# The first MLP product of the context tokens: token tiles as stationary operand, W1 moving in split tiles of 512 columns, results turned by PE transposes

## Chip, core and metric

The kernel runs on one core of a Trainium2 chip. The metric is device microseconds of one launch. The kernel before took 2586.35 us as the median of three runs (2584.51 to 2587.87). A difference of about 0.2%, some 5 us, is what a measurement of this kernel can tell from no change.

## What is computed

One layer of a diffusion backbone on 128 context tokens (one tile of 128 rows) and 2048 latent tokens (16 tiles). A DeltaNet and gMLP mixer comes first; it is not touched. Behind it stands the MLP, for context and latent tokens with the same weights:

```python
def block(x, s0, mod, n_chunks, ...):
    ...
    x = x + ga1 * o
    h = rmsnorm(x, norm_ffn_l) * (1.0 + sc2) + sh2
    x = x + ga2 * (jnp.square(jax.nn.relu(h @ w_ff1_l)) @ w_ff2_l)
    return x, s_new
```

`w_ff1` (W1) is 1024 x 4096 and `w_ff2` is 4096 x 1024, all in 32-bit floats. The change is about `square(relu(h @ w_ff1))` for the 128 context rows.

## The kernel before

All engines work on tiles of 128 partitions by 512 floats (256 KB), nearly all from one pool of 49 buffers (`wp`). A product that must be exact to about 32 bits is made of three matmuls (`mm3`, lines 238 to 244): each operand is split into a rounded part H (a cast on ScalarE, ACT) and a rest L (a subtraction on VectorE, DVE), and H by H, H by L and L by H are added up in PSUM. Lines 242, 243 and 244 of the profile are these three. PSUM is eight banks of 512 floats, handed out by `bank()`.

The first MLP product of the latent tokens is a two-by-two block scheme with seven products instead of eight, over `ORDER = (1, 5, 6, 7, 3, 2, 4)`. The 16 latent tiles form two halves of 8; a half's activations lie in seven `hop` tiles of 2 MB, one for each product, which move through the PE as the 512-wide operand; `hop_next` loads one in two transfers of 1 MB. W1 goes through the PE as the stationary operand. A `Unit` holds 256 columns of W1 (four raw tiles `raw[i, kh]` of 256 KB, read in rows of 512 bytes) and makes seven `step(o)`s of 12 matmuls each. There are 16 units for each half. `seq` lists the 224 steps; the first two and last two units of a half run interleaved. At position `p` the program emits the loads of the unit at `p + 14`, the splits of its weights at `p + 6` (`LEAD`), and the step of `p`. `half` is the position at which the second half begins; around it the seven `hop` tiles are exchanged, each as soon as the PE has used the old one for the last time. SyncE (SP) issues all these transfers in one queue, in order.

The second half takes the context tokens along: `weights_at`, for four of the seven products (`SINGLE`), emits `Unit.single`, which multiplies the unit's raw W1 tiles, unsplit, with the 128 context columns `x0` as the moving operand. A `T.matmul` on unsplit 32-bit floats runs as two matmul instructions, so the 256 calls are 512 instructions of 128 columns in the profile (line 1646). `single_out` then takes relu on ACT (line 1652), squares on DVE and stores `z_d[0]`. The result has W1's columns on the partitions, as the second product wants it.

A scheduler orders each engine's instructions when the program is built; `h2_steps` (transposes of line 889) run in the first half.

Behind the second half comes the MLP's second product (`products`, matmuls on `zH` and `zL`). Its first loads are issued from 16 positions before the end of `seq`.

Of the kernel before, what the change touches and what calls it, by code (L numbers as in the profile page):

```python
# [12 lines left out]
AF = mybir.ActivationFunctionType  # L13
ALU = mybir.AluOpType
# [3 lines left out]
P = 128  # L18
D = 1024
KT = D // P  # L20
# [34 lines left out]
NV = 7  # L55
LEAD = 6
ORDER = (1, 5, 6, 7, 3, 2, 4)
SINGLE = {6: (0, 0), 7: (1, 0), 2: (0, 1), 4: (1, 1)}
NK = DFF // P // 2
AHEAD = 3  # L60
WINDOWS = [2.46, 0.03, -0.51, 1.06, -1.61, 18.16, 17.58, 18.3,
# [4 lines left out]
def hybrid_step(  # L66
# [7 lines left out]
    V, A, G, T = nc.vector, nc.scalar, nc.gpsimd, nc.tensor  # L74
    load = nc.sync.dma_start
    store = nc.sync.dma_start
# [10 lines left out]
    def f32(ap):  # L87
        return ap.bitcast(F32)
# [25 lines left out]
    z_d = [dp.tile([4 if a else 1, P, 2, NK, P], F32, name=f"z{a}_d") for a in range(5)]  # L114
# [4 lines left out]
    ident = cp.tile([P, P], F32, name="ident")  # L119
# [69 lines left out]
    def raw_w(src, pool=None, tag="w"):  # L189
        t = (pool or wp).tile([P, 512], F32, tag=tag, name="raw")  # L190
        load(out=t, in_=src)
        return t

    def split_w(raw, scale=None, pool=None, tag="w"):

        h = (pool or wp).tile([P, 512], F32R, tag=tag, name="wH")
        lo = (pool or wp).tile([P, 512], F32R, tag=tag, name="wL")
        if scale is not None:
            A.activation(h, raw, AF.Copy, scale=scale)
            V.scalar_tensor_tensor(out=lo, in0=raw, scalar=scale, in1=f32(h), op0=ALU.mult, op1=ALU.subtract)  # L200
            return h, lo
        A.copy(h, raw)
        V.tensor_tensor(out=lo, in0=raw, in1=f32(h), op=ALU.subtract)
        return h, lo
# [24 lines left out]
    def w512(name, dt=F32):  # L229
        return wp.tile([P, 512], dt, tag="w", name=name)  # L230
# [7 lines left out]
    def mm3(ps, trip, first=True, last=True, more=False):  # L238

        n = len(trip)  # L240
        for i, (lh, ll, rh, rl) in enumerate(trip):
            T.matmul(ps, lh, rh, start=first and i == 0, stop=False, skip_group_check=more)  # L242
            T.matmul(ps, lh, rl, start=False, stop=False, skip_group_check=more)  # L243
            T.matmul(ps, ll, rh, start=False, stop=last and i == n - 1, skip_group_check=more)  # L244
# [51 lines left out]
    with ExitStack() as ph:  # L296
# [8 lines left out]
        def pt():  # L305
            return ppt.tile([P, 512], F32, tag="pt", name="pt", bufs=3)
# [7 lines left out]
        for d in range(2):  # L314
            m = p1.tile([P, P], F32, tag=f"mcum{d}", name=f"mcum{d}", bufs=1)
# [33 lines left out]
        def mod_sum(raws, psum):  # L349

            pm = psum()
            for k in range(KT):
                T.matmul(pm[0:2, :], scond[:, k, :], raws[k], start=k == 0, stop=k == KT - 1)
            row = pf.tile([2, 512], F32, tag="first", name="first", bufs=2)
            A.copy(row, pm[0:2, :])
            return row
# [45 lines left out]
        r0 = mod_sum(m0, pm1)  # L402
# [15 lines left out]
        ps = pt()  # L418
# [4 lines left out]
        for t in BLOCKS[0]:  # L423
            x = p1.tile([P, D], F32, tag="x", name="x", bufs=3)
# [368 lines left out]
        for bi in range(len(BLOCKS)):  # L793
# [8 lines left out]
            for n, (gi, h) in enumerate(order):  # L802
                u = us[n] if bi == 0 and n < 3 else feature_tile(blk, bi, gi, h)
# [150 lines left out]
    def hop_next():  # L954
        g, o = hop_order.pop(0)
        hop[g, o] = t = hop_tile(F32R, o in ORDER[:2])
        for k in range(0, 4, 2):
            load(out=f32(t)[:, k : k + 2], in_=hop_d[g, o][:, k : k + 2])


    with ExitStack() as ph:
# [246 lines left out]
        units = [unit(t, 0) for t in range(NT)] + [unit(t, 1) for t in [0] + list(range(NT - 1, 0, -1))]  # L1208
# [218 lines left out]
        for i, u in enumerate(units):  # L1427
            w = p2 if i <= NT else p3
# [7 lines left out]
            n = len(u["prep"])  # L1436
# [6 lines left out]
            if i >= NT:  # L1443
                at(i, lambda u=u: o_loads(u))
                first, second = o_steps(u)
# [21 lines left out]
        for j, st in enumerate(flat[:NF]):  # L1467
            g, k = divmod(j, KT + 1)
# [53 lines left out]
    def bank():  # L1522
        return psq.tile([P, 512], F32, tag="f", name="f", bufs=8)

    def add(out, a, b, op=ALU.add):
        V.tensor_tensor(out=out, in0=a, in1=b, op=op)  # L1526

    def split4(src, name="w"):

        h = wp.tile([P, 4, P], F32R, tag="w", name=name + "H")  # L1530
        lo = wp.tile([P, 4, P], F32R, tag="w", name=name + "L")
        A.copy(h, src)  # L1532
        add(lo, src, f32(h), ALU.subtract)
        return h, lo

    def as4(t):
        return t.rearrange("p (a d) -> p a d", a=4)


    NP = DFF // 256  # L1540
    x0 = []

    class Unit:

# [37 lines left out]
        def product(self, o, onto=None):  # L1582
            if onto is None:
                self.ps[o] = bank()
            (h, lo), m = self.w[o], hop[self.g, o]
            mm3(self.ps[onto or o], [(h[:, kp, :], lo[:, kp, :], m[:, :, 0, kp, :], m[:, :, 1, kp, :]) for kp in range(4)],
                first=onto is None, more=onto is not None)
# [50 lines left out]
                rl2(c, c)  # L1638
                self.out(1, 0, c)

        def single(self, o, ps, i, first, last):

            m, kh = SINGLE[o]
            c = (2 * i + m) * P
            for kp in range(4):
                T.matmul(ps[:, c : c + P], self.raw[m, kh][:, kp, :], x0[kh][:, kp, :], start=first and kp == 0,  # L1646
                         stop=last and kp == 3)

    def single_out(units, ps):
        n = 256 * len(units)  # L1650
        z = w512("z0")
        A.activation(z[:, :n], ps[:, :n], AF.Relu)
        add(z[:, :n], z[:, :n], z[:, :n], ALU.mult)
        for i, u in enumerate(units):
            store(out=z_d[0][0, :, :, u.jp, :], in_=z[:, i * 256 : i * 256 + 256].rearrange("p (a t) -> p a t", a=2))

    def first_load():
        for i in range(2):
            r = as4(w512("x0"))
            load(out=r, in_=h2_d[0][:, i * 4 : i * 4 + 4, :])  # L1660
            x0.append(r)


    pairs = [(9 + 2 * i, 10 + 2 * i) for i in range(4)] + [(1 + 2 * i, 2 + 2 * i) for i in range(4)]
# [23 lines left out]
    def fetch(src, name="r2"):  # L1688
        t = w512(name)
        load(out=t, in_=src)  # L1690
        return t
# [177 lines left out]
    def t_ahead(n, upto):  # L1869
        while n < len(products) and len(traws) < min(upto, NK):  # L1870
            traws.append(fetch(moving(products[n][0], len(traws)), "traw"))

    def t_next(n, k):

        if n < len(products):
            t_ahead(n, k + 4)
            tiles[n].append(t_build(traws[k], k))
            if k == NK - 1:
                traws.clear()

    def s_next(m, loads):
        if m < len(todo):
            if loads:
                raws[m] = s_load(*todo[m][1:])
            else:
                sops[m] = s_build(*raws.pop(m))
# [4 lines left out]
    units = {n: Unit(n) for n in range(2 * NP)}  # L1891
# [2 lines left out]
        seq += [(o, n, b) for o in ORDER for n in b]  # L1894
    begun = set()

    bank0 = {}

    def weights_at(p):
        if p < len(seq):  # L1900
            o, n, b = seq[p]
            units[n].weights(o)
            if n >= NP and o in SINGLE:
                first, last = o == 6 and n == b[0], o == 4 and n == b[-1]
                if first:
                    bank0[b[0]] = bank()
                units[n].single(o, bank0[b[0]], b.index(n), first, last)
                if last:
                    single_out([units[m] for m in b], bank0[b[0]])

    def loads_at(p):
        if p < len(seq) and seq[p][1] not in begun:
            begun.add(seq[p][1])
            units[seq[p][1]].loads()
# [3 lines left out]
    for p in range(LEAD):  # L1918
        if p < 5:
            hop_next()  # L1920
        weights_at(p)
    half = [p for p, e in enumerate(seq) if e[1] == NP][0]
    later = []
    for j, t in enumerate(range(8, -1, -1)):
        st = h2_steps(t, bank, lambda: w512("junk"), w512)
        p = 10 + 19 * j // 2
        later += [(p + (-4, 0, 1, 2, 4, 5)[k] if k < 6 else p + 2 * k - 6, st[k]) for k in range(len(st))]
    later.sort(key=lambda e: e[0])
    last = len(seq) - 16
    for p, (o, n, b) in enumerate(seq):  # L1930
        u = units[n]
        loads_at(p + LEAD + 8)
        weights_at(p + LEAD)
        while later and later[0][0] <= p:
            later.pop(0)[1]()
        if p == half - 20:
            first_load()
        u.step(o)
        if half - 11 <= p < half + 3 and (half - p) % 2:
            hop_next()  # L1940
        e = p - last
        if e >= 0 and e % 2:
            if e // 2 == 0:
                for m in range(AHEAD):
                    s_next(m, True)
                t_ahead(0, 4)
            elif e // 2 < 5:
                for k in range(4 * (e // 2) - 4, 4 * (e // 2)):
                    t_next(0, k)
                if e // 2 <= AHEAD:  # L1950
                    s_next(e // 2 - 1, False)
                    s_next(AHEAD + e // 2 - 1, True) if e // 2 < 3 else None
# [4 lines left out]
    for m, (n, i, u, q) in enumerate(todo):  # L1957
# [6 lines left out]
        if q == 0:  # L1964
            ps = bank()
# [6 lines left out]
        h, lo = sops.pop(m)  # L1972
        if m >= len(todo) - 4:
# [8 lines left out]
            if q == 3:  # L1982
                rest[0](ps, 0)
                ps = bank()
# [12 lines left out]
        if i in (1, 5, 6) and mm < 28:  # L1997
            while pending and mm >= pending[0][0] + 2:
                _, k, r = pending.pop(0)
# [60 lines left out]
```

## Time and profile before

| | us |
|---|---|
| median of three runs | 2586.35 |
| the profiled execution, device time | 2589.03 |
| its span, first to last instruction | 2587.1 |
| PE busy in it | 2547.4 |
| DVE busy | 1805.3 |
| ACT busy | 1221.0 |

The stages that matter: the first half of the first MLP product runs from 1246.9 us of the span on, the second half from about 1540 us to 1923 us, the second product to the end. "L1646" is line 1646 of the kernel; `f` is a PSUM bank, `hop` the activations, `wH` and `wL` split weights. A window row gives, for each engine, busy us and in brackets the number of instructions; then the granted TensorE clock as a share of the full one, the share of the time in which the DMA engines were busy, and GB/s.

### The profile page before, as it was taken

The page shows a single profiled execution, that of the slowest core. Times are in us where ns is not written, and L with a number is a line of the kernel's source. Part 1 is how long each engine was busy: PE and PEld are TensorE (multiplying, and loading weights), DVE is VectorE, ACT ScalarE, POOL GpSimd, SP SyncE. Part 2 cuts the span into 40 slices and gives each one's busy share as a digit, 9 for nine tenths or more (in the row PEclk, how much of TensorE's full clock was granted, in tenths as well). Part 3 has the DMA queues.
Part 4 walks back from the last instruction along what each step waited for, and adds up shares of the span by engine and source line. Part 5 has one row for each costly group of instructions (what it writes and reads, how often), then busy time and mean ns, then how long its engine had stood idle before and what let it go on. Part 6 is the DMA issues. An engine that isn't in the chain of part 4 may idle for free.

```text
span 2587.1 us, 44754 instructions
## 1 busy us (share of the span) xinstructions
PE 2547.4 (98%) x15556; PEld 2154.5 (83%) x15556; DVE 1805.3 (70%) x3738; ACT 1221.0 (47%) x3051; POOL 233.7 (9%) x448
## 2 busy tenths in 40 slices
PE   9999999999999999999999999999999999999998
PEld 5899998788888787788888888888888888888887
DVE  5867757766677878886678876666665557784875
ACT  4755556555555667764345543333342432342442
POOL 3112212111111111210000000000000000000000
PEclk9999999999999999999999999999999999999999
DMA  8977737644454656885868788444479979786683
GB/s 287 300 219 213 211 111 253 229 154 155 144 160 151 215 177 235 281 275 183 280 205 252 230 289 293 122 115 118 120 239 368 345 257 327 266 257 204 223 266 112
DMA packets 494695, 571.88 MB, mean 221 GB/s; under 512 B 35124, under 2 KB 297564, under 8 KB 490886
## 3 DMA queue, kind: packets, MB, share of 16 engines
q1 hardware_dynamic: 494470, 569.04, 67.8%
q8 instruction: 122, 2.00, 0.3%
q14 instruction: 103, 0.84, 0.1%
HBM read 389.23 MB, written 179.67 MB: 220 GB/s over the span
## 4 chain that ended last, share of the span: by engine, by line
PE 86%; DMA 6%; DVE 5%; ACT 2%; issue 1%; SPq 0%; POOL 0%; POOLq 0%; DVEq 0%; ACTq 0%
PE f L242 16%; PE f L244 16%; PE f L243 16%; PE pj L242 7%; PE pj L244 6%; PE pj L243 6%; PE pd L1011 4%; PE f L1646 2%; PE pm L242 1%; PE pm L244 1%; PE pm L243 1%; PE pt L626 1%; DMA QK<-qk_d 1%; DMA raw<-in_w_mod_dram 1%; DMA hop_d<-opL 1%
## 5 line engine op out<-in xcount | busy, mean ns | idle before, releaser
L242 PE MATMUL f<-hop,zH 128*128 128x512 f32 (+1 forms) x976 | 376.2, 386 | 1.2 <-ACT zH L1532 1.2
L243 PE MATMUL f<-hop,zH 128*128 128x512 f32 (+1 forms) x976 | 376.1, 386 | 0.0
L244 PE MATMUL f<-hop,zL 128*128 128x512 f32 (+1 forms) x976 | 376.1, 386 | 0.0
L242 PE MATMUL f<-hop,wH 128*128 128x512 f32 x896 | 355.2, 397 | 0.1
L243 PE MATMUL f<-hop,wH 128*128 128x512 f32 x896 | 349.0, 390 | 0.0
L244 PE MATMUL f<-hop,wL 128*128 128x512 f32 x896 | 347.9, 390 | 0.0
L1532 ACT CAST zH<-zraw 128x512 fp32r<-128x512 f32 x240 | 146.4, 620 | 284.6 <-DMA zraw<-s_d 86.9
L242 PEld LDWEIGHTS f<-hop,zH 128*128 128x128 f32 x976 | 183.3, 188 | 38.5 <-ACT zH L1532 1.6
L244 PEld LDWEIGHTS f<-hop,zL 128*128 128x128 f32 x976 | 183.3, 188 | 37.3 <-DVE zL L1526 0.4
L243 PEld LDWEIGHTS f<-hop,zH 128*128 128x128 f32 x976 | 183.3, 188 | 36.9 <-issue 0.2
L1526 DVE TENSOR_TENSOR zL<-zraw,zH 128x512 fp32r<-128x512 f32 x240 | 162.6, 687 | 72.2 <-ACT zH L1532 55.1
L244 PEld LDWEIGHTS f<-hop,wL 128*128 128x128 f32 x896 | 168.2, 188 | 35.3
L242 PEld LDWEIGHTS f<-hop,wH 128*128 128x128 f32 x896 | 168.5, 188 | 32.8 <-issue 0.5
L243 PEld LDWEIGHTS f<-hop,wH 128*128 128x128 f32 x896 | 168.5, 188 | 32.3
L242 PE MATMUL pj<-kH,wH 128*128 128x386 f32 (+2 forms) x568 | 190.5, 338 | 1.3 <-ACT junk L602 1.1
L243 PE MATMUL pj<-kL,wH 128*128 128x386 f32 (+2 forms) x568 | 189.5, 335 | 0.5 <-POOL kL L511 0.5
L244 PE MATMUL pj<-kH,wL 128*128 128x386 f32 (+2 forms) x568 | 189.7, 335 | 0.0
L185 POOL TENSOR_TENSOR r<-rsq,nhalf 128x1 f32<-128x1 f32 (+1 forms) x37 | 25.1, 679 | 1418.0 <-DVE rsq L184 1418.0
L572 DVE SCALAR_TENSOR_TENSOR cv<-pj,vec,cv 128x384 f32<-128x384 f32 (+2 forms) x164 | 87.0, 539 | 52.7 <-ACT cv L569 51.4
L242 PEld LDWEIGHTS pj<-kH,wH 128*128 128x128 f32 x568 | 107.0, 189 | 4.6 <-issue 2.6
L1532 ACT CAST wH<-s 128x512 fp32r<-128x512 f32 x96 | 59.4, 621 | 105.5 <-DVE s L1526 103.5
L243 PEld LDWEIGHTS pj<-kL,wH 128*128 128x128 f32 x568 | 107.4, 189 | 1.4 <-POOL kL L511 0.8
(410 smaller groups left out, 5703.9 us busy)
## 6 DMA issues: line engine op xcount, KB each, us to landing
zraw<-z_d SPq DMA_DIRECT2D x212, 256.0 KB
raw<-in_w_ff_dram SPq DMA_DIRECT2D x128, 256.0 KB
hop<-hop_d SPq DMA_DIRECT2D x28, 1024.0 KB
z_d<-c SPq DMA_DIRECT2D x96, 256.0 KB
zraw<-s_d SPq DMA_DIRECT2D x96, 256.0 KB
raw<-in_w_mod_dram SPq DMA_DIRECT2D x80, 256.0 KB
r<-in_w_ff_dram SPq DMA_DIRECT2D x80, 256.0 KB
s_d<-s SPq DMA_DIRECT2D x64, 256.0 KB
```

What stands on the lines that cost most here:

```text
L185: G.tensor_tensor(out=out, in0=t[:np_, :n], in1=nhalf[:np_, :n], op=ALU.pow)
L242: T.matmul(ps, lh, rh, start=first and i == 0, stop=False, skip_group_check=more)
L243: T.matmul(ps, lh, rl, start=False, stop=False, skip_group_check=more)
L244: T.matmul(ps, ll, rh, start=False, stop=last and i == n - 1, skip_group_check=more)
L572: V.scalar_tensor_tensor(out=cv[:, o : o + m], in0=ps[:, s + sh : s + sh + m], scalar=convw[:, w, j : j + 1], in1=cv[:, o : o + m], op0=AL ...
L626: T.matmul(ps[:, i * P : (i + 1) * P], kTt[:, i * P : (i + 1) * P], rhs[:, i * P : (i + 1) * P], start=True, stop=True)
L1011: T.matmul(p[:, h, :], lhs[:, h, :], rhs[:, h, :], start=True, stop=True)
L1526: V.tensor_tensor(out=out, in0=a, in1=b, op=op)
L1532: A.copy(h, src)
L1646: T.matmul(ps[:, c : c + P], self.raw[m, kh][:, kp, :], x0[kh][:, kp, :], start=first and kp == 0, stop=last and kp == 3)
```

## The change

`Unit.single`, `single_out` and `SINGLE` go, and with them line 1646. In their place the context tokens get a product of their own over the whole of W1. `first_load` now splits `x0` into H and L (four tiles that stay). `context_steps(m)` handles one 128 x 512 tile of W1, `m = 8 fb + k` (eight blocks `fb` of 512 columns, eight tiles `k` of 128 rows):

- `fetch`: load the tile from DRAM once more (rows of 2 KB), 10 positions ahead;
- `split`: cast on ACT, rest on DVE, 4 positions ahead;
- `product`: three matmuls with the context's H or L as stationary operand and the W1 tile as 512 moving columns; at `k = 7`, relu of the whole bank on ACT;
- `turn`, 2 positions later and once for each block: four PE transposes of 128 x 128 into a second bank, a square on ACT and two stores.

One `m` comes every one and a half positions, from `half - 6` on, so that the last product stands at `half + 88` of 112 positions.

```diff
-        def single(self, o, ps, i, first, last):
-            m, kh = SINGLE[o]
-            c = (2 * i + m) * P
-            for kp in range(4):
-                T.matmul(ps[:, c : c + P], self.raw[m, kh][:, kp, :], x0[kh][:, kp, :], ...)
-    def single_out(units, ps):
-        A.activation(z[:, :n], ps[:, :n], AF.Relu)
-        add(z[:, :n], z[:, :n], z[:, :n], ALU.mult)
...
     def first_load():
         for i in range(2):
             r = as4(w512("x0"))
             load(out=r, in_=h2_d[0][:, i * 4 : i * 4 + 4, :])
-            x0.append(r)
+            h, lo = split4(r, "x")
+            x0.extend((h[:, k, :], lo[:, k, :]) for k in range(4))
+
+    def context_steps(m):
+        fb, k = divmod(m, KT)
+        u = first_tile
+        def fetch():
+            u["raw", m] = raw_w(w_ff1[0, k * P : (k + 1) * P, fb * 512 : fb * 512 + 512])
+        def split():
+            u["w", m] = split_w(u.pop(("raw", m)))
+        def product():
+            if k == 0:
+                u["ps"] = bank()
+            mm3(u["ps"], [x0[k] + u.pop(("w", m))], first=k == 0, last=k == KT - 1)
+            if k == KT - 1:
+                u["r", fb] = w512("r0")
+                A.activation(u["r", fb], u["ps"], AF.Relu)
+        def turn():
+            r, ps, z = u.pop(("r", fb)), bank(), w512("z0")
+            for j in range(4):
+                T.transpose(ps[:, j * P : (j + 1) * P], r[:, j * P : (j + 1) * P], ident)
+            A.activation(z, ps, AF.Square)
+            for j in range(2):
+                store(out=z_d[0][0, :, :, 2 * fb + j, :], ...)
+        return [(-10, fetch), (-4, split), (0, product)] + ([(2, turn)] if k == KT - 1 else [])
...
-                units[n].single(o, bank0[b[0]], b.index(n), first, last)
-                if last:
-                    single_out([units[m] for m in b], bank0[b[0]])
...
+    for m in range(8 * KT):
+        firsts += [(half - 6 + m * 3 // 2 + e, m, f) for e, f in context_steps(m)]
```

What this does to the order is shown at three places, all shortly behind the start of the second half. On the PE, before, at the product 7 of the first unit (`hop_20701`) a group of the removed matmuls follows 12 of line 242 to 244:

```order
L242 MATMUL f_20964<-hop_20701,wH_20821 128x512
L243 MATMUL f_20964<-hop_20701,wH_20821 128x512
L244 MATMUL f_20964<-hop_20701,wL_20822 128x512
L1646 MATMUL f_20762<-x0_20329,raw_20501 128x128 x4
L242 MATMUL f_21004<-hop_20701,wH_20846 128x512
```

In the changed program, at the end of the same product (`hop_20748`), the eighth tile of the first context block (`wH_20905`, `wL_20906`, cut from `raw_20720`) goes through, and product 3 of the first unit (`hop_20816`) is next:

```order
L243 MATMUL f_21044<-hop_20748,wL_20884 128x512
L241 MATMUL f_20712<-wH_20905,xH_20335 128x512
L242 MATMUL f_20712<-wL_20906,xH_20335 128x512
L243 MATMUL f_20712<-wH_20905,xL_20336 128x512
L241 MATMUL f_20943<-hop_20816,wH_20939 128x512
```

The context's matmuls now need a freshly loaded and split tile, where they needed a raw tile of the unit that had long been there. (Lines of the changed kernel are one lower up to line 1540, so 241 to 243 are `mm3`.)

On ACT, at that same place, before:

```order
L1600 COPY x_20867<-f_20854 128x512
L1532 CAST wH_20873<-s_20704 128x512
L1604 COPY p5_20890<-f_20877 128x512
L1532 CAST wH_20893<-s_20729 128x512
L1604 COPY p5_20910<-f_20897 128x512
```

and in the changed program, where line 201 is the cast of a context tile:

```order
L201 CAST wH_20905<-raw_20720 128x512
L1531 CAST wH_20913<-d_20911 128x512
L1600 COPY x_20930<-f_20917 128x512
L1531 CAST wH_20939<-s_20751 128x512
L1604 COPY p5_20956<-f_20943 128x512
L201 CAST wH_20958<-raw_20780 128x512
L1531 CAST wH_20965<-s_20782 128x512
L1604 COPY p5_20982<-f_20969 128x512
```

A cast of a context tile, which waits for a transfer, has moved in ahead of the casts and copies that the next `hop` products wait for: `p5_20956` must be copied out before product 3 of the first unit adds onto that bank, `p5_20982` before that of the second.

On SP's queue, in the changed program, from the sixth exchanged `hop` tile on (before, the rows of line 190 are absent):

```order
L957 DMA hop_20870<-hop_1_2_d_91 128x2048 x2
L190 DMA raw_20684<-in_w_ff1_dram 128x512
L1590 DMA z4_d_101<-c12_20705 128x4x128
L957 DMA hop_20935<-hop_1_4_d_93 128x2048
L1593 DMA s10_d_102<-s1_20709 128x4x128
L190 DMA raw_20720<-in_w_ff1_dram 128x512
L957 DMA hop_20935<-hop_1_4_d_93 128x2048
L1590 DMA z4_d_101<-c12_20738 128x4x128
L1593 DMA s10_d_102<-s1_20742 128x4x128
L1590 DMA z3_d_100<-c11_20769 128x4x128
L190 DMA raw_20780<-in_w_ff1_dram 128x512
```

The tiles `k = 6`, `k = 7` and the first one of the second block (`raw_20684`, `raw_20720`, `raw_20780`) stand in the queue between the last `hop` tiles: counted from the first exchanged `hop` tile they are transfers number 35, 39 and 44, behind 18.6, 20.5 and 22.5 MB with their own. Four loads of a unit that stood between the halves of the last `hop` tile now come behind these.

More of the change, by code (lines that the diff above doesn't have):

```diff
@@ L57 @@
 ORDER = (1, 5, 6, 7, 3, 2, 4)
-SINGLE = {6: (0, 0), 7: (1, 0), 2: (0, 1), 4: (1, 1)}
 NK = DFF // P // 2
@@ L1541, in hybrid_step @@
     x0 = []
+    first_tile = {}
     class Unit:
@@ L1639, in step @@
                 self.out(1, 0, c)
-        def single(self, o, ps, i, first, last):
-            m, kh = SINGLE[o]
-            c = (2 * i + m) * P
-            for kp in range(4):
-                T.matmul(ps[:, c : c + P], self.raw[m, kh][:, kp, :], x0[kh][:, kp, :], start=first and kp == 0,
-                         stop=last and kp == 3)
-    def single_out(units, ps):
-        n = 256 * len(units)
-        z = w512("z0")
-        A.activation(z[:, :n], ps[:, :n], AF.Relu)
-        add(z[:, :n], z[:, :n], z[:, :n], ALU.mult)
-        for i, u in enumerate(units):
-            store(out=z_d[0][0, :, :, u.jp, :], in_=z[:, i * 256 : i * 256 + 256].rearrange("p (a t) -> p a t", a=2))
     def first_load():
@@ L1660, in first_load @@
             load(out=r, in_=h2_d[0][:, i * 4 : i * 4 + 4, :])
-            x0.append(r)
+            h, lo = split4(r, "x")
[20 more added lines that the diff above has]
+            for j in range(2):
+                store(out=z_d[0][0, :, :, 2 * fb + j, :], in_=z[:, j * 256 : j * 256 + 256].rearrange("p (a t) -> p a t", a=2))
+        return [(-10, fetch), (-4, split), (0, product)] + ([(2, turn)] if k == KT - 1 else [])
     pairs = [(9 + 2 * i, 10 + 2 * i) for i in range(4)] + [(1 + 2 * i, 2 + 2 * i) for i in range(4)]
@@ L1895, in hybrid_step @@
     begun = set()
-    bank0 = {}
     def weights_at(p):
@@ L1902, in weights_at @@
             units[n].weights(o)
[L1903 to L1906, printed above, removed]
-                units[n].single(o, bank0[b[0]], b.index(n), first, last)
-                if last:
-                    single_out([units[m] for m in b], bank0[b[0]])
     def loads_at(p):
@@ L1929, in hybrid_step @@
     last = len(seq) - 16
+    firsts = []
+    for m in range(8 * KT):
+        firsts += [(half - 6 + m * 3 // 2 + e, m, f) for e, f in context_steps(m)]
+    firsts.sort(key=lambda e: e[0])
     for p, (o, n, b) in enumerate(seq):
@@ L1938, in hybrid_step @@
         u.step(o)
+        while firsts and firsts[0][0] <= p:
+            firsts.pop(0)[2]()
         if half - 11 <= p < half + 3 and (half - p) % 2:
```

## The prediction

> **What bounds the kernel now.** I read the page first, then busy time by stage, then the PE's timeline and the DMA traffic around the start of the second half. The page:
>
> ```profile
> span 2587.1 us, 44754 instructions
> PE 2547.4 (98%) x15556; PEld 2154.5 (83%) x15556; DVE 1805.3 (70%) x3738; ACT 1221.0 (47%) x3051; POOL 233.7 (9%) x448
> PE 86%; DMA 6%; DVE 5%; ACT 2%; issue 1%; SPq 0%; POOL 0%; POOLq 0%; DVEq 0%; ACTq 0%
> ```
>
> The PE makes 86% of the chain that ended last. In the stages that the change touches, and the two behind, it is fuller still:
>
> ```profile
> 1246.90:1540.00 293.10, 292.97 (x1327) 242.47 (x1326) 226.80 (x385) 150.51 (x315) 5.73 (x9) 1.00 0.80 254
> 1540.00:1905.00 365.00, 365.00 (x1867) 311.39 (x1867) 235.68 (x370) 121.85 (x223) 0.00 (x0) 1.00 0.54 167
> 1923.20:2200.00 276.80, 275.61 (x1240) 226.82 (x1239) 164.57 (x259) 91.37 (x159) 0.00 (x0) 1.00 0.93 325
> 2200.00:2587.00 387.00, 380.34 (x1724) 316.71 (x1722) 265.02 (x449) 136.29 (x262) 11.91 (x17) 1.00 0.67 221
> ```
>
> From 1540 to 1905 us, where all of the removed matmuls lie, the PE has no idle time at all, at a granted clock of 1.00; DVE is busy 65%, ACT 33%, DMA 54% of the time. So a microsecond taken from the PE's queue there is a microsecond of span, as long as nothing new makes it wait; and behind it the PE loses only 1.2 us until 2200 us.
>
> **What is removed.** A busy time of a matmul overlaps the next one's, so I take distances between starts:
>
> ```profile
> 1558.94 1.05 PE L1646 MATMUL f<-x,raw 128*128 128x128 f32 x8
> ...
> 1563.38 0.48 PE L242 MATMUL f<-hop,wH 128*128 128x512 f32 x1
> ...
> 1566.19 1.05 PE L1646 MATMUL f<-x,raw 128*128 128x128 f32 x8
> 1569.82 0.39 PE L242 MATMUL f<-hop,wH 128*128 128x512 f32 x1
> ...
> 1575.03 0.39 PE L244 MATMUL f<-hop,wL 128*128 128x512 f32 x1
> 1575.26 1.05 PE L1646 MATMUL f<-x,raw 128*128 128x128 f32 x8
> L1646 PE MATMUL f<-x,raw 128*128 128x128 f32 x512 | 67.5, 274 | 0.0
> ```
>
> From 1569.82 to 1575.26 run 24 wide matmuls: 0.2267 us each. Between 1558.94 and 1566.19 lie two groups of line 1646 and 24 wide ones: 7.25 - 24 x 0.2267 = 1.81, so 0.905 us for a group of 8 instructions. 512 instructions are 64 groups: **57.9 us** go from the PE. With them go small relus and squares (5.8 and 5.7 us on ACT and DVE), which nobody waits long for.
>
> **What is added on the PE.** 64 tiles x 3 = 192 matmuls, 128 rows by 512 columns in split parts: the same form as lines 242 to 244 on `hop`, only with the roles changed. 192 x 0.2267 = **43.5 us**. Then 8 x 4 = 32 transposes of 128 x 128 floats; line 889 does the same:
>
> ```profile
> 1502.66 1.03 PE L889 MATMUL f<-ident,x 128*128 128x128 f32 x8
> 1503.45 0.48 PE L242 MATMUL f<-hop,wH 128*128 128x512 f32 x1
> 1503.76 0.40 PE L243 MATMUL f<-hop,wH 128*128 128x512 f32 x1
> 1503.99 0.39 PE L244 MATMUL f<-hop,wL 128*128 128x512 f32 x1
> L889 PE MATMUL f<-ident,x x72: 270/272/273, 1285.6 to 1503.4; 128*128 128x128 f32 x72
> ```
>
> From 1502.66 to 1503.99 are 8 transposes and two wide matmuls: 1.33 - 0.45 = 0.88, 0.11 us each, 32 x 0.11 = **3.5 us**. The PE's queue thus gets shorter by 57.9 - 43.5 - 3.5 = **10.9 us**, if the PE never waits.
>
> The Trainium skill speaks against this term: "TensorE: Matmul & The Clock Gate", Part 4 (PE-mode transpose), gives about 275 ns for a 128 x 128 transpose in one kernel's context, which would make 8.8 us of these 32. The trace disagrees as long as transposes come in runs: 0.11 us from start to start, though one's recorded duration is 272 ns.
>
> **What is added elsewhere.**
>
> ```profile
> L1532 ACT CAST wH<-raw 128x512 fp32r<-128x512 f32 x49 | 28.8, 617 | 1.6 <-DMA raw<-in_w_ff_dram 1.6
> L1526 DVE TENSOR_TENSOR wL<-raw,wH 128x512 fp32r<-128x512 f32 x52 | 35.3, 686 | 33.1 <-ACT wH L1532 33.1
> ```
>
> 64 splits cost 64 x 0.617 = 39.5 us on ACT and 64 x 0.686 = 43.9 us on DVE, 16 relus and squares of 512 some 10 us more on ACT. Over a stage of some 357 us DVE comes to (235.7 - 5.7 + 43.9) / 357 = 77%, ACT to 46%. The PE hides this: a split is emitted 4 positions, at least 11 us of PE time, ahead of its product. If that cover went, the price would be that of the third rival. Splitting `x0` costs two casts and two subtractions, 2.6 us, in the first half, beside 20 positions of PE work. The first half keeps its PE order but for the first products.
>
> 64 transfers of 256 KB are 16.8 MB. Most of them fall where DMA is at leisure; those of the start do not:
>
> ```profile
> 1540.00:1560.00 20.00, 20.00 (x97) 16.79 (x97) 17.11 (x28) 7.37 (x13) 0.00 (x0) 1.00 1.05 393
> 1560.00:1580.00 20.00, 20.00 (x105) 17.11 (x105) 11.19 (x18) 6.19 (x11) 0.00 (x0) 1.00 1.02 360
> 1640.00:1680.00 40.00, 40.00 (x211) 34.26 (x210) 26.18 (x41) 11.99 (x22) 0.00 (x0) 1.00 0.41 116
> 1900.00:1910.00 10.00, 10.00 (x54) 8.57 (x53) 8.88 (x15) 5.95 (x11) 0.00 (x0) 1.00 0.17 49
> 1525.50 0.80 SPq L958 DMA_DIRECT2D hop<-hop_d  x2
> 1574.35 2.57 SPq L958 DMA_DIRECT2D hop<-hop_d  x1
> 1582.44 0.69 SPq L958 DMA_DIRECT2D hop<-hop_d  x1
> GB/s 83 311 399 358 288 344 346 345 332 415 430 420 363 300 327 410 420 425 404 415 420 344 388 383 376 386 356 427 421 441 349 345 221 220 386 279 345 361 397 334
> DMA packets 17908, 22.62 MB, mean 358 GB/s; under 512 B 699, under 2 KB 16113, under 8 KB 16113
> ```
>
> (The last two rows are the DMA view of 1525.5 to 1588.7 us, in 40 slices and as a whole.) While the seven `hop` tiles are exchanged the DMA engines are busy all the time, at 358 GB/s; the context's first nine tiles stand in that queue. Before, this exchange made no PE wait, because each tile landed well ahead of its use.
>
> **The wait this adds.** In the changed program transfer 44 (first tile of the second block, `raw_20780`) has 22.5 MB up to and with itself: 22.5 / 0.358 = 63 us behind 1525.5, and 1 us from the last byte to the semaphore, an estimate: about 1589.5. Behind its cast on ACT stand the cast and the copy (`p5_20982`) for product 3 of the second unit, behind its subtraction on DVE that product's rest: two casts of 0.62 and a subtraction of 0.69, about 2 us with the handovers, so 1591.5.
>
> When would the PE be there? Before, the second half's first `hop` product began at 1563.38, by counting the order. Three groups ahead of it go (2.7 us), six context matmuls come (1.4): 1562.0. Up to product 3 of the second unit run 96 `hop` and 18 context matmuls, 114 x 0.2267 = 25.8: 1587.9, its first use of the rest 0.4 later, 1588.3. The PE waits **about 3.3 us** in all. Part of it comes one product sooner, behind tile `k = 7` (transfer 39, 20.5 MB, about 1583.7, with its product due at 1584.4 and five casts and copies in a row behind it); that is not added, since the second landing sets the end. The wait moves one for one with the landing: at the 420 GB/s that the same exchange reaches in its best slices nothing is left of it, at 330 GB/s it is 8 to 9 us. These are the ends; I take 358 GB/s, the mean of this very stretch.
>
> The last `hop` tile itself has 21.5 MB before it instead of 22.3 and is needed some 12 us after the end of that wait. Behind 1600 us the tiles are fetched some 27 us of PE time ahead, with DMA at 41% before; no further wait is counted. The end of the stage has room as well: the last product stands 24 positions before the end, and the loads for the next stage, which get some 5 us less time, find DMA at 17% at 1900.
>
> **The sum.** 10.9 - 3.3 = 7.6 us. The profiled execution took 2589.0 us of device time, 1.9 above its span and 2.7 above the median. So 2581.4 for it, and **2578.8 us** for the median.
>
> **The rivals.**
>
> *No wait at the exchange*: the queue drains faster or the scheduler's order has more slack than I read from it. For it: before, every one of these tiles came in time. Then the whole 10.9 us stay: 2575.5. Chance 0.13.
>
> *A longer wait*, over 5.7 us, at the same place: the DMA engines are at their limit there, ACT and DVE work in order, and each late tile holds up what is behind it. A wait of 8.5 us gives 2584.0. Chance 0.18.
>
> *Every context tile stops the PE* (slower). The change puts 64 more casts and subtractions, each behind a transfer, in front of work that the PE waits for, in queues that run in order; if each made the PE wait 0.4 us, 64 x 0.4 = 25.6 us would be lost, for 2586.35 - 10.9 + 25.6 = 2601. It decides from 10.9 / 64 = 0.17 us a tile. For it: DVE at 77%. Against it: before, casts on raw tiles waited 1.6 us for DMA in the whole stage, and the lead of 11 us is many times a split. Chance 0.08.
>
> *The transposes do not overlap*: in fours, behind an ACT result, each takes its recorded 0.272 us, 8.7 us instead of 3.5: 2584.0 with the wait. Chance 0.04, since line 889 in the same stage shows 0.11. The page named above would have this one.
>
> *The change doesn't do what it says*: matmuls with a W1 tile as the moving operand take two passes, as line 1646's did. Then 43.5 us more, 2622. Nothing in the rows speaks for it; 0.02.
>
> **How the numbers follow.** My forecast has 0.55 (a wait between some 0.5 and 5.7 us, 2576 to 2581.2). A measurement can tell about 0.2%, 5.2 us, from no change. Faster by more: forecast and no wait, 0.68. Within: longer wait and slow transposes, 0.22. Slower: 0.10. The range goes from 2574.5, the full gain and a microsecond of spread, to 2586.0, a wait of some 10.5 us; beyond are the slower cases and little more.
>
> **What would show it.** No line 1646; 192 matmuls `f<-wH` and `f<-wL` at 0.227 us from start to start; 32 transposes at 0.11; PE idle of 2 to 5 us between about 1584 and 1592 us of the span, released by ACT copies or DVE rests at line 1525, with casts of line 201 waiting for DMA just before; none after 1600. The stage from there to the second product is shorter by some 9 us at equal idle. Idle time spread over the stage would mean the third rival; a start distance over 0.227 the last; a wait for a `hop` tile instead of an ACT or DVE result would mean that I read the exchange wrongly.

## The result, and the profile after

The changed kernel took 2580.91 us as the median of 14 runs (2575.13 to 2585.76), the kernel before 2586.34 us in 14 runs beside it (2581.58 to 2588.33): a ratio of 0.9979 with a 95% interval of 0.9971 to 0.9987. That is 5.4 us faster, just over the 0.2% that counts, with an interval that reaches below it; the forecast for the median was 2578.8 us. The profiled execution took 2580.59 us of device time, against the 2581.4 forecast for it.

The page of the changed kernel, the rows that stood in the prediction for the kernel before:

```profile
span 2578.7 us, 44496 instructions
PE 2539.4 (98%) x15268; PEld 2139.2 (83%) x15268; DVE 1836.7 (71%) x3790; ACT 1259.7 (49%) x3119; POOL 234.2 (9%) x448
PE 89%; DMA 5%; DVE 4%; ACT 1%; issue 1%; POOL 0%; SPq 0%; POOLq 0%; DVEq 0%; ACTq 0%
```

The PE is still the bound. Its busy time fell by 8.0 us and the span by 8.4, while DVE got 31 us and ACT 39 us more work. The windows of the stage (columns as before: busy us of PE, PEld, DVE, ACT and POOL, then clock, DMA share, GB/s):

```profile
1580.00:1600.00 20.00, 19.41 (x88) 15.50 (x87) 12.93 (x22) 11.61 (x22) 0.00 (x0) 1.00 1.08 351
1600.00:1700.00 100.00, 100.00 (x447) 82.78 (x446) 80.58 (x130) 47.04 (x87) 0.00 (x0) 1.00 0.68 200
1800.00:1890.00 90.00, 90.00 (x402) 74.53 (x401) 64.99 (x103) 38.38 (x70) 0.00 (x0) 1.00 0.55 164
```

Of these windows only 1580 to 1600 us, at the end of the exchange of the `hop` tiles, has a PE that is not full. Behind it DVE is busy 81% and 72% of the time, and the PE does not wait.

How long the whole product took is read from the first and last starts of its groups. The rows of the PSUM tile `f`, before and after (count, shortest, middle and longest duration in ns, first and last start, shapes):

```profile
L242 PE MATMUL f<-hop,zH x976: 278/389/499, 1923.4 to 2579.8; 128*128 128x512 f32 x189, 128*128 128x256 f32 x7
L242 PE MATMUL f<-hop,wH x896: 387/389/481, 1247.1 to 1922.7; 128*128 128x512 f32 x180
```

```profile
L241 PE MATMUL f<-hop,zH x976: 278/389/499, 1915.0 to 2571.4; 128*128 128x512 f32 x189, 128*128 128x256 f32 x7
L241 PE MATMUL f<-hop,wH x896: 389/389/504, 1248.2 to 1914.3; 128*128 128x512 f32 x180
L241 PE MATMUL f<-wH,xH x64: 389/389/481, 1549.9 to 1851.3; 128*128 128x512 f32 x64
L1670 PE MATMUL f<-ident,r x32: 270/272/273, 1593.3 to 1857.7; 128*128 128x128 f32 x32
its engine sat idle before it (us, times) until:
  ACT zH L1531: 1.2, 1
  ACT p L1604: 0.6, 1
```

From its first matmul to the first of the second product (`zH`) the first MLP product took 1923.4 - 1247.1 = 676.3 us before and 1915.0 - 1248.2 = **666.8 us** after, 9.5 us less. The mixer ahead of it, which is the same, took 1.1 us more in this execution. That is the 8.4 us of the span. That the profiled execution came within 0.8 us of its forecast is therefore partly luck: the stage gained 1.9 us more than forecast, and the mixer took back 1.1. The stage gained more than the forecast 7.6 us because the wait at the exchange was much shorter than the 3.3 us of the sum. This is where it stands, on the PE and on ACT:

```profile
1586.20 0.39 PE L243 MATMUL f<-wH,xL 128*128 128x512 f32 x1
1587.18 0.50 PE L241 MATMUL f<-hop,wH 128*128 128x512 f32 x1 [0.59 <-ACT p L1604]
...
1590.06 0.46 PE L241 MATMUL f<-hop,wH 128*128 128x512 f32 x1
```

```profile
1582.98 0.62 ACT L201 CAST wH<-raw 128x512 fp32r<-128x512 f32 x1 [1.16 <-PE f L242]
1585.02 0.62 ACT L1531 CAST wH<-d 128x512 fp32r<-128x512 f32 x1 [1.42 <-DVE d L1525]
1585.54 0.58 ACT L1600 COPY x<-f 128x512 f32<-128x512 f32 x1
1586.02 0.62 ACT L1531 CAST wH<-s 128x512 fp32r<-128x512 f32 x1
1586.54 0.59 ACT L1604 COPY p<-f 128x512 f32<-128x512 f32 x1
1588.34 0.62 ACT L201 CAST wH<-raw 128x512 fp32r<-128x512 f32 x1 [1.21 <-DMA raw<-in_w_ff_dram]
1588.86 0.61 ACT L1531 CAST wH<-s 128x512 fp32r<-128x512 f32 x1
1589.38 0.58 ACT L1604 COPY p<-f 128x512 f32<-128x512 f32 x1
```

The chain is the forecast one: the cast of tile `k = 7` at 1582.98 us (the row puts its wait down to the PE; but the last update of the transfer's semaphore stands at 1582.90 in the trace, 0.08 us before the cast, as it does before the cast of 1588.34), behind it the casts and copies, and `p` at 1586.54, for which the PE waits. The next PE start comes at 1587.18 instead of 1586.43, so 0.75 us are lost. The second landing, on which the forecast wait rested, is the cast at 1588.34. The copy behind it lets the PE go on at 1590.06, and by twelve matmuls after 1587.18 the PE was due at 1589.90. It costs 0.16 us.

### The profile page after: what moved, and what is told of

It is laid out like the page before. It is cut to its first block, busy times and chain, and to the rows that moved or that the text cites. A ratio compares the mean times of both kernels' runs of the same rounds, so it can differ in the third digit from the quotient of the medians.

```text
span 2578.7 us, 44496 instructions
## 1 busy us (share of the span) xinstructions
PE 2539.4 (98%) x15268; PEld 2139.2 (83%) x15268; DVE 1836.7 (71%) x3790; ACT 1259.7 (49%) x3119; POOL 234.2 (9%) x448
## 4 chain that ended last, share of the span: by engine, by line
PE 89%; DMA 5%; DVE 4%; ACT 1%; issue 1%; POOL 0%; SPq 0%; POOLq 0%; DVEq 0%; ACTq 0%
PE f L241 17%; PE f L242 17%; PE f L243 17%; PE pj L241 7%; PE pj L243 7%; PE pj L242 7%; PE pd L1010 5%; PE pm L241 1%; PE pm L243 1%; PE pm L242 1%; DMA raw<-in_w_mod_dram 1%; PE pt L625 1%; PE pt L584 1%; PE pd L1093 1%; DMA hop_d<-opL 1%
## 5 line engine op out<-in xcount | busy, mean ns | idle before, releaser
L243 PE MATMUL f<-hop,zL 128*128 128x512 f32 (+1 forms) x976 | 376.1, 386 | 0.0
L243 PE MATMUL f<-hop,wL 128*128 128x512 f32 x896 | 347.5, 389 | 0.0
L243 PEld LDWEIGHTS f<-hop,zL 128*128 128x128 f32 x976 | 183.3, 188 | 37.3 <-DVE zL L1525 0.4
L243 PEld LDWEIGHTS f<-hop,wL 128*128 128x128 f32 x896 | 168.2, 188 | 35.3
L243 PE MATMUL pj<-kH,wL 128*128 128x386 f32 (+2 forms) x568 | 189.7, 335 | 0.0
L202 DVE TENSOR_TENSOR wL<-raw,wH 128x512 fp32r<-128x512 f32 x120 | 81.7, 688 | 40.0 <-ACT wH L201 36.6
```

## The experiments

Two accounts stood against each other. **Wait**: what the stage doesn't gain of the 10.9 us is lost where the context's first tiles share the DMA queue with the `hop` tiles, and this loss grows with the bytes in that queue. **Slack**: tiles and handovers had room, and what is missing in the time lies elsewhere. The stage below is always the first MLP product, from first to first start as above.

### The context product later, its first tiles earlier, and twice as much in the queue

Four kernels on one chip, with the kernel before (2587.34 us, 26 runs). `e_same` is the changed kernel again.

> The changed kernel once more, as the control. Two theories. Exchange theory: the PE's queue got 10.9 us shorter, and the only new cost is a wait of a few us while the hop tiles are exchanged, which differs from run to run with the DMA rate; this profile shows idle time there alone, and the time is 2577 to 2583 us. Elsewhere theory: the exchange costs 1.4 us as in the first profile, and some 4 us of the median are lost in another stage (second product, or the steady part of the second half): its start-to-start times show them.

```diff
 e_late
-        firsts += [(half - 6 + m * 3 // 2 + e, m, f) ...]
+        firsts += [(half + 10 + m * 3 // 2 + e, m, f) ...]
```

> The whole context product starts 16 positions later (half + 10 instead of half - 6), so that its first tile is fetched behind the last hop tile. Exchange theory: no PE wait at the exchange, about 2575.5 us. Elsewhere theory: about 2580.9. A wait near 1900 us, where the product now ends 8 positions before the stage does, would be a cost of its own.

```diff
 e_early
-        firsts += [(half - 6 + m * 3 // 2 + e, m, f) ...]
+        firsts += [(half - 17 if e == -10 and m < 9 else half - 6 + m * 3 // 2 + e, m, f) ...]
```

> The first nine context tiles of W1 are all fetched at position half - 17, so that they stand ahead of all but the first exchanged hop tile in SP's queue. Exchange theory: no PE wait there, 10.9 us under before, about 2575.5 us, and less spread. Elsewhere theory: as the control, about 2580.9, or only 1.4 us less. If the hop tiles, now 6.6 us later, come too late: PE waits for a hop tile and no gain over the control.

```diff
 e_twice
         def fetch():
             u["raw", m] = raw_w(...)
+            if m < 9:
+                raw_w(w_ff1[0, k * P : (k + 1) * P, 512 + fb * 512 : 512 + fb * 512 + 512])
```

> Each of the first nine context tiles is followed by a second transfer of 256 KB into a tile that nobody reads: 2.36 MB more in the queue of the exchange, 6.6 us at 358 GB/s. Exchange theory: the PE's wait there grows one for one, from 1.4 to about 7 or 8 us, 2586 to 2588 us. If the exchange had slack: no change, 2581.

| | median us (range, runs) | ratio to before, 95% | stage, us |
|---|---|---|---|
| `e_same` | 2580.69 (2574.19 to 2582.52, 9) | 0.9972, 0.9962 to 0.9982 | 667.9 |
| `e_late` | 2576.96 (2573.25 to 2585.03, 8) | 0.9967, 0.9956 to 0.9977 | 666.7 |
| `e_early` | 2579.41 (2575.82 to 2584.37, 9) | 0.9973, 0.9964 to 0.9983 | 666.9 |
| `e_twice` | 2590.41 (2585.05 to 2595.87, 11) | 1.0012, 1.0001 to 1.0023 | 675.9 |

The waits of the PE from 1500 to 1930 us (in all, times, longest) in `e_same`, `e_late`, `e_early` and `e_twice`:

```profile
PE f L241 <- ACT p L1604: 0.9, 2, 0.6
```

```profile
PE f L242 <- DVE wL L202: 0.4, 1, 0.4
```

```profile
PE f L241 <- ACT wH L1531: 0.7, 1, 0.7
```

```profile
PE f L241 <- ACT p L1604: 2.1, 1, 2.1
PE f L241 <- ACT wH L201: 1.8, 2, 1.6
PE f L241 <- ACT wH L1531: 0.6, 1, 0.6
PE f L242 <- DVE wL L202: 0.4, 2, 0.2
```

`e_same` has the same wait of 0.6 us at the same place as the first profile. (Its other wait, 0.3 us at 1515.6 us, lies ahead of the exchange: a copy on ACT stands behind the cast of `x0`, which waits for its transfer. `e_same2` below has one like it, 0.35 us. The prediction had put the splitting of `x0` at nothing in its sum.) `e_late` and `e_early` move it (to a context tile's rest at 1611 us, to an ACT cast at 1591) but leave 0.4 and 0.7 us; their medians and the one of `e_same` are not told apart by the intervals. Neither is free of waits or at 2575.5 us, as the first account had it, and their stages are those of the changed kernel at its best (666.8 us). `e_twice` is the strong test: nine tiles of 256 KB more in the queue, 2.36 MB or some 6.3 us at the rate of the exchange, bring 4.9 us of waits around this place and take back the whole gain. Its median is 2.4 to 4.4 us above the expected times. Its stage is 9.1 us longer than that of the changed kernel. By the distances between starts it is lost between 1567 and 1597 us. The idle time explains 4.3 us of it; where the rest lies shows in the next experiment.

### A third of the context's matmuls

If the PE comes to the exchange sooner, it must wait longer there, as long as the DMA queue stays as it is. One matmul for each tile instead of three takes 128 x 0.2267 = 29.0 us from the PE's queue. Eight tiles are multiplied ahead of the wait, so 16 of these matmuls, 3.6 us, lie ahead of it (the expectation counts 12).

```diff
 e_third
-            mm3(u["ps"], [x0[k] + u.pop(("w", m))], first=k == 0, last=k == KT - 1)
+            wh, wl = u.pop(("w", m))
+            T.matmul(u["ps"], x0[k][0], wh, start=k == 0, stop=k == KT - 1)
```

> Only H by H of the context product (its two products with a rest are left out): 128 wide matmuls less, 128 x 0.2267 = 29.0 us. If each of them lies on the path, the first MLP product (first hop matmul to first of the second product, 666.8 and 667.9 us in two profiles of the changed kernel) takes 637.8 us when the exchange has slack left, and 640.5 us when the wait there is set by the landing of the tiles: the PE then comes 12 matmuls, 2.7 us, sooner to the same transfer and waits for it.

One run: 2551.37 us, beside 2588.19 for the kernel before; the stage took 646.2 us, against 666.8 - 29.0 = 637.8 without further waits. The direction is that of the wait, and it is larger than the 640.5 expected. The PE's timeline there, and windows of it:

```profile
1576.18 0.39 PE L243 MATMUL f<-hop,wL 128*128 128x512 f32 x1
1577.99 0.50 PE L1663 MATMUL f<-wH,xH 128*128 128x512 f32 x1 [1.42 <-ACT wH L201]
1581.51 0.79 PE L241 MATMUL f<-hop,wH 128*128 128x512 f32 x1 [3.02 <-ACT p L1604]
1582.11 0.63 PE L242 MATMUL f<-hop,wH 128*128 128x512 f32 x1
...
1585.94 0.43 PE L242 MATMUL f<-hop,wH 128*128 128x512 f32 x1
```

```profile
1579.20:1586.00 6.80, 4.49 (x11) 3.53 (x12) 5.24 (x9) 6.25 (x13) 0.00 (x0) 0.50 1.06 325
1586.00:1590.00 4.00, 4.00 (x22) 3.31 (x20) 3.28 (x5) 1.05 (x3) 0.00 (x0) 1.00 1.06 346
```

The waits of the stage come to 5.0 us instead of 0.6. The PE idles 1.42 and 3.02 us, and the granted clock is 0.50 from 1579.2 to 1586.0 us: from 1582.11 to 1585.94 nine matmuls go through at 0.426 us instead of 0.227, which with the slow start before them costs another 2 us. `e_twice` shows the same behind its wait of 2.06 us:

```profile
1590.20:1597.00 6.80, 4.74 (x12) 3.69 (x12) 3.70 (x6) 4.88 (x10) 0.00 (x0) 0.50 1.06 333
```

So a wait there costs its own length only as long as it is short.

The other part is that the queue did not stay as it was. The edit takes out matmuls only, but the scheduler orders the program anew, and the second half of the last `hop` tile, 1 MB, now stands ahead of the context tile `k = 7`. SP's queue in the changed kernel, then in `e_third` (line 957 loads `hop`, line 190 the context tile):

```profile
1569.68 1.08 SPq L957 DMA_DIRECT2D hop<-hop_d  x1
...
1572.09 3.34 SPq L190 DMA_DIRECT2D raw<-in_w_ff_dram  x1
1575.48 0.43 SPq L957 DMA_DIRECT2D hop<-hop_d  x1
```

```profile
1561.30 0.37 SPq L957 DMA_DIRECT2D hop<-hop_d  x1
...
1563.30 0.32 SPq L957 DMA_DIRECT2D hop<-hop_d  x1
...
1564.74 5.16 SPq L190 DMA_DIRECT2D raw<-in_w_ff_dram  x1
```

`e_twice` has the same exchange of places, beside eight of its extra tiles ahead of `k = 7`. When this tile landed, by the last update of its semaphore in the traces, and when product 3 of the first unit started on the PE:

| | `k = 7` landed, us behind the first exchanged transfer | PE's start, behind this landing | PE's start, behind the first `hop` matmul |
|---|---|---|---|
| after, `e_same`, `e_same2` | 56.1, 56.2, 56.3 | 4.28, 4.28, 4.28 | 339.0, 340.1, 339.4 |
| `e_third` | 58.9 | 4.22 | 341.8 |
| `e_twice` | 63.4 | 4.21 | 346.0 |

The PE's start keeps to the landing within 0.1 us, whether the landing is later by 2.8 or by 7.3 us. That settles the mechanism, and it explains both stages. In `e_third` the start comes 2.8 us later than in the changed kernel with 3.6 us less work ahead of it: 6.4 us, and 2.0 at the half clock make the 8.4. In `e_twice` it comes 7.0 us later, and 2.1 behind it make the 9.1. The idle times are smaller than these sums, since a start behind a wait comes 0.15 to 0.3 us later than the idle time says, as in the row of 1587.18 above, and some starts around the waits are late.

### The transposes

```diff
 e_noturn
-            r, ps, z = u.pop(("r", fb)), bank(), w512("z0")
-            for j in range(4):
-                T.transpose(ps[:, j * P : (j + 1) * P], r[:, j * P : (j + 1) * P], ident)
-            A.activation(z, ps, AF.Square)
+            r, z = u.pop(("r", fb)), w512("z0")
+            A.activation(z, r, AF.Square)
```

> The 32 transposes are left out (the square is taken from the untransposed tile). At 0.11 us each the first MLP product gets 3.5 us shorter than 666.8, at about 275 ns each 8.8 us shorter.

One run: 2576.94 us. The stage took, by these rows of `e_noturn`, 1910.6 - 1247.6 = 663.0 us:

```profile
L241 PE MATMUL f<-hop,zH x976: 278/389/499, 1910.6 to 2567.4; 128*128 128x512 f32 x189, 128*128 128x256 f32 x7
L241 PE MATMUL f<-hop,wH x896: 388/389/501, 1247.6 to 1909.9; 128*128 128x512 f32 x180
```

That is 3.8 us less than the 666.8 us with the 32 transposes, 0.12 us each; against the two other profiles of the changed kernel (667.2 and 667.9) it would be up to 4.9, still far from 8.8. The changed kernel's PE timeline at the first four shows the smaller figure:

```profile
1593.33 0.60 PE L1670 MATMUL f<-ident,r 128*128 128x128 f32 x4
1593.69 0.48 PE L241 MATMUL f<-wH,xH 128*128 128x512 f32 x1
1594.00 0.40 PE L242 MATMUL f<-wL,xH 128*128 128x512 f32 x1
1594.24 0.40 PE L243 MATMUL f<-wH,xL 128*128 128x512 f32 x1
```

Without the transposes L243 would have started two matmuls behind 1593.33, at 1593.78; it starts at 1594.24, so four cost 0.46 us, although the group row records 272 ns for each.

### How much the same program differs from itself

The kernel before, profiled three more times.

> The kernel before, once more, for where its own executions differ. Theory: the first 1247 us (mixer, the same program in both kernels) vary by some us from execution to execution, and the profile of before that was read lay at their long end; from the first matmul on a hop tile to the first of the second product it is 676.3 us again, the second product 656.6 us again to within a few us. Rival: the mixer takes 1247 us again, and the second product 656.6 us exactly, so that the 0.5 to 2.7 us more of the changed kernel's executions there belong to the change.

> As b1, a third look at the kernel before: the first 1247 us vary by some us, the first MLP product takes 676.3 us; the rival has 1247 us and 656.6 us once more.

> The kernel before against itself in the same call: ratio 1 within 0.1 to 0.2%. Its profile is a fourth look at the mixer (1238.8 to 1247.1 us so far), at the first MLP product (676.3) and at the second (656.6 to 657.4).

`b1` took 2584.72 us and `b2` 2581.23 (one run each), `b3` 2585.89 as the median of 11 runs, a ratio of 1.0003 to the same kernel beside it (0.9994 to 1.0012). By their profiles the stages were:

| | mixer, to the first `hop` matmul | first MLP product | second product, first to last start |
|---|---|---|---|
| before | 1247.1 | 676.3 | 656.4 |
| `b1`, `b2`, `b3` | 1242.0, 1238.8, 1242.0 | 676.3, 676.4, 676.3 | 657.1, 656.8, 658.0 |
| after | 1248.2 | 666.8 | 656.4 |
| `e_same`, `e_same2` | 1241.7, 1245.9 | 667.9, 667.2 | 659.1, 661.7 |

In the kernel before the first MLP product repeats within 0.1 us, in the changed one within 1.1, so its difference can be read from single profiles to about 1 us. The mixer, the same instructions in the same order in all of these rows, differs by 9 us from one execution to another, as much as the stage gained; the second product by up to 5.

### Later and with more lead

`e_late` had left one wait for a tile's rest. With fetches and splits a little further ahead it should go.

```diff
 e_behind
-        return [(-10, fetch), (-4, split), (0, product)] + ...
+        return [(-12, fetch), (-5, split), (0, product)] + ...
...
-        firsts += [(half - 6 + m * 3 // 2 + e, m, f) ...]
+        firsts += [(half + 10 + m * 3 // 2 + e, m, f) ...]
```

> Context product from half + 10 on as in e_late, but each tile fetched 12 positions ahead (instead of 10) and split 5 ahead (instead of 4). If what e_late still lost was its first tiles landing too late, no wait of a context tile or of a hop tile is left, and the first MLP product takes 676.3 - 10.7 = 665.6 us (e_late 666.7, changed kernel 666.8 and 667.9); in time that is 1 to 2 us under the changed kernel, too little to be told apart. Otherwise it stays at 666.7.

> The changed kernel again, beside the kernel before in the same call. By the stage times (first MLP product 9 us shorter, second product up to 2 us longer, mixer the same program) it should be 7 to 9.5 us faster; by the two medians so far 5.4 to 7.2 us. If its mixer is slower though it is the same program, the first hop matmul comes later than in b3 on average.

On one chip, with the kernel before at 2585.34 us (18 runs): `e_behind` 2577.48 (2574.88 to 2579.88, 6 runs), ratio 0.9966 (0.9955 to 0.9978); `e_same2`, the changed kernel a third time, 2577.58 (2575.35 to 2584.01, 7 runs), ratio 0.9969 (0.9958 to 0.9981). In `e_behind` the PE has no idle time from 1500 to 1930 us, and the rows

```profile
L241 PE MATMUL f<-hop,zH x976: 277/389/500, 1909.7 to 2568.5; 128*128 128x512 f32 x189, 128*128 128x256 f32 x7
L241 PE MATMUL f<-hop,wH x896: 387/389/500, 1243.7 to 1909.1; 128*128 128x512 f32 x180
```

give a stage of 666.0 us: 10.3 us shorter than before, with no wait at the exchange. That is the PE's term almost by itself. The version is 0.8 to 1.9 us better in the stage than the three profiles of the changed kernel, too little to show in the medians.

## Why the prediction was right

- **What bounds the kernel**: right. The PE is full before and after, and nearly what goes from its queue goes from the stage.
- **The PE's terms** (57.9 removed, 43.5 and 3.5 added): right. `e_behind` gives 10.3 us where 10.9 was forecast; the transposes cost 3.7 us by the starts around four of them and 3.8 to 4.9 by `e_noturn`, instead of 3.5, the context matmuls have the 0.227 us of the `hop` ones. The rival of slow transposes falls with `e_noturn`. The Trainium skill's figure for a transpose ("TensorE: Matmul & The Clock Gate", Part 4, about 275 ns) is close to what this profile records for one (270 to 273 ns), not to what one costs in a row (0.11 to 0.12 us).
- **The added wait**: the right place, the right cause, but the term was mis-sized: 3.3 us against 0.75 at product 3 of the first unit and 0.16 at that of the second, 0.9 in all. (Its own figures give 1591.5 - 1588.3 = 3.2.) The rate of the transfers failed first. Over the same 63.2 us from the first exchanged `hop` tile on, the DMA view of the changed kernel has

```profile
1526.78 1.09 SPq L957 DMA_DIRECT2D hop<-hop_d  x2
DMA packets 16223, 23.69 MB, mean 375 GB/s; under 512 B 763, under 2 KB 13148, under 8 KB 14427
```

  where the kernel before had 358 GB/s. This is not chance: the four profiles of the kernel before have 356 to 358 in that stretch, the three of the changed one 374 and 375, and `e_late`, with no context tile in the exchange, 354. The prediction carried the rate of one mixture of transfers over to another: four loads in rows of 512 bytes had gone behind the exchange and nine in rows of 2 KB had come in, and the changed kernel moved more bytes in fewer packets (16223 against 17908). That the row length makes the difference is likely, but no run changes it alone. The first tile of the second block landed at 1588.26, 61.5 us behind the first transfer, where the prediction had 63 and 1 (no row gave that 1 us). The PE's go at 1590.06 is thus 63.3 us behind the first transfer instead of 66.0; but the PE needed it 0.4 us sooner than forecast, since it waits with the product's first matmul, for the copy, and not with a later one for the rest: 3.2 - 2.7 + 0.4 = 0.9. With the second landing so early, what held the PE was the tile before it, `k = 7`, with the casts and copies behind it, which the prediction had named and not added.
- **"The wait moves one for one with the landing"**: right for the PE's start, which keeps to the landing of `k = 7` within 0.1 us, but the price of a long wait is higher. Both kernels that made it longer lost another 2 us behind it, by the halved clock; the far end given for the wait (8 to 9 us at 330 GB/s) was too cheap by about as much.
- **No wait behind 1600 us, and the other engines hidden**: right. DVE was forecast at 77% and ACT at 46% of the stage; from 1540 to 1898 us they had 74 and 45%, and the PE was full behind 1600. The rival in which every context tile stops the PE did not come. Only the splitting of `x0` was not quite hidden, with the 0.3 us in two of the three profiles of the changed kernel.
- **From the stage to the median**: the forecast gain of 7.6 us for the kernel came out at 5.4 in the first comparison, and by the ratios at 7.2 and 8.0 us in the two others, around a stage that gained 8.4 to 9.5. What lies between is in the mixer and the second product, where the profiles differ by several us either way with the same code. Whether the changed kernel gives back a part there, or whether these are chance differences of a few profiles, stays open; four profiles of the kernel before and three of the changed one can't tell it. The PE's waits in the second product lean towards the first: they come to 1.2 to 1.7 us in the four profiles of before, to 1.2, 2.3 and 3.7 us in the three of the changed kernel.

## What to carry to other kernels

Where one engine is full, count its queue from start to start in the stage that the change touches; here that came within 0.6 us of 10.9. A wait by a shared DMA queue is worth placing exactly and sizing with its ends, since 5% of transfer rate moved the landing by 2.5 us and 2.4 MB took back the whole gain. A rate that was read from the old kernel belongs to the old mixture of transfers. An edit that takes out matmuls alone can still change the order of the DMA queue, when a scheduler orders the program; compare the queues before reading the difference. To verify a few us, compare the stage between fixed instructions, not the span, when other stages vary by more than the change.

## What was not expected of the hardware

- **Waits of a few us halve the PE's clock behind them.** In `e_third` (1.42 and 3.02 us of idle time within 5 us) and `e_twice` (1.61, 0.22 and 2.06), the granted clock was 0.50 for 6.8 us, of which the PE worked in some 4.5, with matmuls at 0.426 us from start to start; in `e_same2` three waits in the second product (0.74, 0.24 and 1.57 us) did the same for 3.4 us, as these two rows show:

```profile
2470.00:2474.00 4.00, 4.00 (x20) 3.30 (x19) 1.81 (x4) 1.88 (x5) 0.00 (x0) 1.00 0.72 195
2481.40:2484.80 3.40, 3.40 (x10) 2.62 (x9) 3.40 (x7) 1.49 (x3) 0.00 (x0) 0.50 0.81 239
```

  The single waits of 0.6 to 0.7 us in the changed kernel, and those of 1.2 us early in the second product, had no such effect. The Trainium skill ("TensorE: Matmul & The Clock Gate", Part 1) has the half rate after an idle window of about 3.4 us, and the full one after as long a busy one. The stretches of 3.4 us and of twice as much agree; the idle time that led to it was not in one piece here, and in `e_same2` came to 2.6 us within 6.
- **The mixer's time spreads by 9 us** (1238.8 to 1248.2 us) over executions of the same instructions. It builds up at many places; no cause was looked for.
